# Row norm factors of a one-core decoder step: from a short column chain with diagonal products to one wide elementwise chain, with the side work emitted behind it

## The chip, the core and the metric

The kernel runs on one core of a Trainium2 chip. The metric is the device time of one execution in microseconds (us). Three executions of the kernel before took 1776.49, 1781.57 and 1782.59 us; their median, 1781.57 us, is the time before.

## What is computed

One inference step of a one-layer decoder for 512 prompt rows and 32 sample rows of width 1024. Of the reference only the norms matter here, and what stands around them:

```python
def rmsnorm(x, g):
    y = x * lax.rsqrt(jnp.mean(x * x, axis=-1, keepdims=True) + EPS)
    return y * g

ua, va, q, k, v, qi, ki, wi = split_proj(rmsnorm(xp, norm_mix_g) @ w_in)
ya, vn = gmlp_mix(...)                       # spatial gating
yb = dsa_prompt(...)                         # index scores, top-k mask, attention
xp = xp + concatenate([ya, yb]) @ w_out
xp = xp + mem_attend(rmsnorm(xp, norm_mem_g), mk, mv, mem_wq, mem_wo)
xp = xp + peer_apply(rmsnorm(xp, norm_ffn_g), ...)   # product keys, 16384 experts
y  = rmsnorm(xp, final_norm_g)
# the same for the 32 sample rows, with paged caches
```

## The kernel before, in words

Activations lie transposed: features on the 128 partitions (8 tiles, `kt`), rows along the free axis. `project` (L244) multiplies weight tiles with them; each product is three matmuls of split operands (`mm3`, L256 to L260), and each weight tile is first split by ScalarE (L220) and VectorE (L224). Three PSUM buffers (tag `pa`) hold products until `emit` reads them on VectorE.

A norm's gain is folded into the activations (`scaled`, L199 and L200), and the row factor 1/rms is applied when a product is read: `rb`, a tile that holds the factor of each row on every partition, is multiplied in at L410 (first projection), L557 (memory query), L595 and L612 (expert input and expert query). So products may start before `rb` is known, but at most three of them, since none can be read before `rb` is there.

`rb` is worked out five times for many rows: once in `folded` (544 rows, the start of the program) and four times in `norm` within `half` (256 or 288 rows, before the memory attention and before the expert layer, for each half of the rows). Each time:

- `squares4` (L146) squares the eight tiles and adds them over the partitions with ones, four tiles in four strips of 32 partitions: 32 equal rows in each of four strips.
- `turned` (L158) copies that to SBUF (L162) and multiplies with one column of `fold` (L166), which puts the sums of 128 rows on 128 partitions, one column for each 128 rows.
- `row_factors` (L170) first emits side work (`self.tick(self.NORM)`, 12 us worth of it), then copies the columns (L179, L180 or L182), works out the factor on 2 to 5 columns (`rstd`, L116 to L126: VectorE, a square root on ScalarE at L118, VectorE), multiplies the identity with each column (L192), multiplies ones with each of these diagonals (L193), and copies the result to `rb` (L194).

The memory's norm and the sample rows' last norm use `row_factors` as well and are not touched by the change.

Order. Side work (index scores and top-k masks, sample attention, routing) is written as generators. `tick(us)` steps them while main work is emitted, so that the program text mixes them; a scheduler with a simulated timeline then sets each engine's order from that text. An engine runs its list in order. Two places matter below: the first norm, whose ScalarE list also issues the DMAs of the cached index pages (`index_rows`, L1328); and the last one (second half, expert layer), where the side work is the routing of the first 128 rows (`top16`, L933 to L945, on VectorE).

Of the kernel before, what the change touches and what calls it, by code (L numbers as in the profile page):

```python
# [13 lines left out]
ALU = mybir.AluOpType  # L14
# [4 lines left out]
P = 128  # L19
NP = 512  # L20
NS = 32
NT = NP + NS
KT = 8
NB = 3
ND = NB * P
EPS = 1e-6
# [25 lines left out]
class Kernel:  # L52
# [102 lines left out]
                               for c, q in enumerate(self.sq4)])  # L155


    def turned(self, room, st, w):  # L158
        s = self.t(room, [P, w], tag="nsqs", bufs=4)
        n = w // len(st)  # L160
        for i, ps in enumerate(st):
            self.nc.scalar.copy(s[:, i * n : i * n + n], ps[:, :n])  # L162
        o = self.pst("pb")
        for b in range(0, w, P):
            m = min(P, w - b)
            self.nc.tensor.matmul(o[:m, b // P : b // P + 1], s[:, b : b + m], self.fold[:, :1], start=True, stop=True)  # L166
        return o


    def row_factors(self, pool, st, w, rb):  # L170
# [32 lines left out]
    def folded(self, pool, src, gain, w, parts, rb, room=None):  # L203
        nc = self.nc
        st = self.pst("pc") if room else [self.pst("pc") for _ in range(2)]
        for kt in range(KT):
            x = self.t(pool, [P, w], tag="fx", bufs=4 if w > NP else 2)
            nc.sync.dma_start(x, src[:, kt, :])
            g = gain[:, kt : kt + 1]
            for hi, lo, cs in parts:  # L210
                self.scaled(hi[:, kt, :], lo[:, kt, :], x[:, cs], g)
            if room:
                self.squares(room, x, kt, st, w, 1)
            else:
                self.squares4(pool, x, kt, st, w)
        self.row_factors(pool, st if room else self.turned(pool, st, w), w, rb)


    def split(self, hi, lo, x):
# [294 lines left out]
    def half(self, k, pw, h, uT, qT):  # L514
        nc, I = self.nc, self.I
        hh, hl = h
        w = 2 * P + k * NS
# [11 lines left out]
        xT, pm = yield  # L529
        nc.sync.dma_start(xT, I["xT"][:, :, cols])  # L530
        tmp = self.t(pm, [P, 7 * w])
        room = Room(tmp)
        rb = self.t(room, [P, w], tag="nrb")
# [6 lines left out]
        def norm(n, hh=hh, hl=hl):  # L540
            for kt in range(KT):
                self.scaled(hh[:, kt, :], hl[:, kt, :], xT[:, kt, :], self.gains[:, n, kt : kt + 1])
            self.row_factors(pm, self.turned(room, st, w), w, rb)

        st = [self.pst("pc")]
        self.project(pw, I["wO"], range(8), part, residual)
        yield
        norm(1)
        yield
        mst = ExitStack()  # L550
# [13 lines left out]
        for h in range(4):  # L564
            ps = self.pst("pa")
# [4 lines left out]
        pm = yield  # L570
        if not k:
            tmp = self.t(pm, [P, 7 * w])
        room = Room(tmp)
        rb = self.t(room, [P, w], tag="nrb")
        st = [self.pst("pc")]
        self.project(pw, I["wMO"], range(8), part, residual, kts=4)
        yield
        if k:
            nc.scalar.dma_start(self.x2[:, :, P:], xT[:, :, loc])
            nc.vector.tensor_copy(self.s_x, xT[:, :, 2 * P :])  # L580
        else:
            nc.scalar.dma_start(self.x2[:, :, :P], xT[:, :, P:])
            for kt in range(KT):
                self.natural(self.g_acc[:, kt, :], xT[:, kt, :P])
            norm(2)
        if k:
            pf = self.pool("pa_fold", stack=mst)
            fold = [self.t(pf, [P, KT, w], F32R) for _ in range(2)]
            part = [(*fold, cols)]
            norm(2, *fold)  # L590
# [1288 lines left out]
```

## Time and profile before

| | |
|---|---|
| runs | 1776.49, 1781.57, 1782.59 us |
| profiled execution | 1771.42 us, of which the span of the profile is 1769.7 us |
| TensorE (PE) busy | 1647.2 us, 93% of the span |
| VectorE (DVE) busy | 1476.1 us, 83% |
| ScalarE (ACT) busy | 863.9 us, 49% |
| granted TensorE clock | 0.966 of full speed on average |

The profiled execution lies 10.15 us below the median of the runs. The page's busy shares are averages over stages; the stages around the five norms have to be read one by one.

### The profile page before, as it was taken

Reading aid. Unit: us, or ns where it says so; the run is one execution under the profiler, and the core shown is the slowest. Engines: PE = TensorE matmul, PEld = TensorE weight load, DVE = VectorE, ACT = ScalarE, POOL = GpSimd, SP = SyncE. Lnnn points to the kernel's source line nnn. Section 1 sums busy time; section 2 is a strip of 40 time slices with the busy share of each in tenths; the row PEclk is TensorE's granted clock in tenths of the full one; section 3 lists DMA queues with packets and bytes.
Section 4 is the critical chain, followed back from the end, with each engine's and each line's share of the span. In section 5 each row is a group of like instructions: output and inputs, shape, how many; then the busy total and the mean of one; then the engine's idle time right before and its main releaser. Section 6 shows DMA issues by size and latency. Waiting matters only on the chain.

```text
span 1769.7 us, 29580 instructions
## 1 busy us (share of the span) xinstructions
PE 1647.2 (93%) x10238; PEld 1454.7 (82%) x10238; DVE 1476.1 (83%) x3654; ACT 863.9 (49%) x1585; POOL 499.2 (28%) x437
## 2 busy tenths in 40 slices
PE   5999879989997997999899998999999999999996
PEld 4879847879877896899889987888788888888885
DVE  4486989657669999999999975899897988878888
ACT  4246675866444336664774773333443333333333
POOL 2011024310000144232123222343333434345343
PEclk8999869999998998999999999999999999999998
DMA  6423236565754597999688779899998999999986
GB/s 210 116 77 116 79 91 209 179 211 157 229 168 137 168 360 277 328 340 335 211 297 323 268 276 298 277 346 328 374 350 303 372 358 324 354 328 326 362 304 241
DMA packets 195205, 460.33 MB, mean 260 GB/s; under 512 B 17976, under 2 KB 98616, under 8 KB 193648
## 3 DMA queue, kind: packets, MB, share of 16 engines
q1 hardware_dynamic: 127968, 239.59, 40.5%
q0 software_dynamic: 53072, 207.71, 33.1%
q10 hardware_dynamic: 14016, 11.15, 2.0%
q8 instruction: 80, 1.31, 0.3%
q14 instruction: 69, 0.57, 0.1%
HBM read 416.11 MB, written 42.05 MB: 259 GB/s over the span
## 4 chain that ended last, share of the span: by engine, by line
PE 66%; DVE 17%; DMA 6%; issue 6%; ACT 4%; POOL 1%; ACTq 0%; SPq 0%; POOLq 0%; DVEq 0%
PE t L260 20%; PE t L258 20%; PE t L259 20%; DVE t L224 3%; DMA t<-in_u,t 2%; DVE t L1744 2%; DMA t<-in_uT 1%; POOL t L1285 1%; PE t L654 1%; DMA wd<-t 1%; DVE t L942 1%; DVE t L937 1%; ACT t L220 1%; DVE t L945 1%; DVE t L933 1%
## 5 line engine op out<-in xcount | busy, mean ns | idle before, releaser
L260 PE MATMUL t<-t,t 128*128 128x384 f32 (+3 forms) x2544 | 867.6, 345 | 26.5 <-DVE t L224 26.0
L259 PE MATMUL t<-t,t 128*128 128x384 f32 (+3 forms) x2544 | 866.0, 342 | 0.0
L258 PE MATMUL t<-t,t 128*128 128x384 f32 (+3 forms) x2544 | 777.5, 345 | 12.4 <-ACT t L220 10.5
L220 ACT CAST t<-t 128x1024 fp32r<-128x1024 f32 (+4 forms) x512 | 418.5, 842 | 680.3 <-PE t L259 487.7
L224 DVE TENSOR_TENSOR t<-t,t 128x1024 fp32r<-128x1024 f32 (+4 forms) x512 | 487.5, 962 | 123.9 <-ACT t L220 120.4
L260 PEld LDWEIGHTS t<-t,t 128*128 128x128 f32 x2544 | 484.3, 191 | 76.0 <-DVE t L224 34.9
L258 PEld LDWEIGHTS t<-t,t 128*128 128x128 f32 x2544 | 484.2, 191 | 54.6 <-ACT t L220 15.3
L259 PEld LDWEIGHTS t<-t,t 128*128 128x128 f32 x2544 | 485.2, 191 | 39.9 <-issue 7.1
L1285 POOL DMA_INDIRECT t<-in_u,t x160 | 201.1, 1257 | 499.3 <-DVE t L1744 256.5
L1285 POOL DMA_INDIRECT t<-in_v,t x160 | 211.7, 1323 | 301.4 <-DVE t L1749 232.4
L1749 DVE SCALAR_TENSOR_TENSOR t<-t,t,t 128x1024 f32<-128x1024 f32 x160 | 204.7, 1279 | 3.9 <-DMA t<-in_v,t 3.0
L1744 DVE SCALAR_TENSOR_TENSOR t<-t,t 128x1024 f32<-128x1024 f32 x160 | 193.9, 1218 | 12.9 <-DMA t<-in_u,t 12.8
L1090 ACT ACTIVATE t<-t 128x512 f32<-128x512 f32 x96 | 96.9, 1147 | 28.5 <-DMA wd<-t 24.2
L1285 POOL DMA_INDIRECT t<-in_cK,t x32 | 31.4, 982 | 163.9 <-PE t L1504 86.6
L1226 DVE TENSOR_TENSOR t<-t,t 128x352 f32<-128x352 f32 x128 | 66.4, 520 | 7.2 <-DMA t<-gd 3.6
L1106 ACT ACTIVATE t<-t 128x384 f32<-128x384 f32 x128 | 62.2, 486 | 15.0 <-PE t L260 9.2
L1080 ACT ACTIVATE t<-t,t 128x128 f16<-128x128 f16 x192 | 58.8, 395 | 7.3 <-DVE t L1076 5.1
L704 ACT ACTIVATE t<-t,t 128x384 f32<-128x384 f32 x64 | 42.7, 667 | 31.8 <-DVE t L701 19.9
L1087 PE MATMUL t<-t,t 128*128 128x128 f16 x384 | 52.8, 225 | 4.8 <-DVE t L1077 2.6
L1088 PE MATMUL t<-t,t 128*128 128x128 f16 x384 | 51.2, 225 | 1.6 <-DVE t L1082 1.2
L1285 POOL DMA_INDIRECT t<-in_cV,t x32 | 34.2, 1069 | 56.2 <-PE t L1561 33.0
L1087 PEld LDWEIGHTS <-t 128*128 128x128 f16 x384 | 36.5, 100 | 12.0 <-issue 5.3
(400 smaller groups left out, 1416.6 us busy)
## 6 DMA issues: line engine op xcount, KB each, us to landing
t<-in_uT SPq DMA_DIRECT2D x128, 512.0 KB, 5.9
t<-in_v SPq DMA_DIRECT2D x128, 512.0 KB, 6.6
wd<-t POOLq DMA_DIRECT2D x11, 2048.0 KB, 9.1
t<-wd SPq DMA_DIRECT2D x32, 704.0 KB, 8.0
gd<-t SPq DMA_DIRECT2D x56, 192.0 KB, 4.4
t<-gd SPq DMA_DIRECT2D x56, 192.0 KB, 7.5
t<-in_wA SPq DMA_DIRECT2D x19, 512.0 KB, 5.6
t<-in_wO SPq DMA_DIRECT2D x16, 512.0 KB, 4.1
```

Of the source, the lines that this page charges most:

```text
L220: self.nc.scalar.copy(hi, x)
L224: self.pin_v = self.nc.vector.tensor_tensor(lo, x, hi, ALU.subtract)
L258: mm(out, ah, bh, start=first, stop=False)
L259: mm(out, ah, bl, start=False, stop=False)
L260: self.pin = mm(out, al, bh, start=False, stop=last)
L1087: nc.tensor.matmul(o, oj[:, x, :], oh[:, x, :], start=True, stop=False)
L1090: nc.scalar.activation(wb[:, :, t : t + 4].rearrange("p i t -> p t i"), ps.rearrange("p (t i) -> p t i", t=4), AF.Copy, scale=1.0 / 2048.0)
L1106: nc.scalar.activation(G, ps, AF.Gelu_apprx_tanh)
L1226: nc.vector.tensor_tensor(q(w)[:, : 4 * NB - 1], self.wp[:, :, i % 4, :], q(G)[:, : 4 * NB - 1], ALU.mult)
L1285: self.nc.gpsimd.indirect_dma_start(out=out, out_offset=None, in_=src, in_offset=bass.IndirectOffsetOnAxis(ap=ix, axis=0))
L1744: nc.vector.scalar_tensor_tensor(r, r, 1.0, hf, ALU.mult, ALU.mult, accum_out=a[:, k : k + 1])
L1749: nc.vector.scalar_tensor_tensor(acc, r, a[:, k : k + 1], acc, ALU.mult, ALU.add)
```

## The change

`turned` goes, and with it `row_factors` for these five norms. `wide_factors` copies the squares' sums as before, multiplies them with a full square of ones (one product of up to 288 columns: it adds the 4 x 32 rows, so every partition holds 32 times the sum of each row), and works out the factor elementwise on all 128 partitions and all columns: a scale and add that reads PSUM, a square root on ScalarE, a reciprocal, a square on ScalarE, and two fused steps of Newton's correction. There are no diagonals and no copy to `rb`; the chain writes `rb` itself. For the 544 rows of the first norm it runs twice, on 272 columns each. `tick(NORM)` stands behind the chain instead of in front of it.

```diff
-    def turned(self, room, st, w):
+    def wide_factors(self, room, st, w, rb):
+        nc = self.nc
         s = self.t(room, [P, w], tag="nsqs", bufs=4)
+        v = self.t(room, [P, w], tag="nsqs", bufs=4)
+        t = self.t(room, [P, w], tag="nsqs", bufs=4)
         n = w // len(st)
         for i, ps in enumerate(st):
-            self.nc.scalar.copy(s[:, i * n : i * n + n], ps[:, :n])
-        o = self.pst("pb")
-        for b in range(0, w, P):
-            m = min(P, w - b)
-            self.nc.tensor.matmul(o[:m, b // P : b // P + 1], s[:, b : b + m], self.fold[:, :1], start=True, stop=True)
-        return o
+            c = slice(i * n, i * n + n)
+            nc.scalar.copy(s[:, c], ps[:, :n])
+            o = self.pst("pb")
+            nc.tensor.matmul(o[:, :n], self.ones, s[:, c], start=True, stop=True)
+            self.factors(v[:, c], t[:, c], o[:, :n], NS, rb[:, c])
+        self.tick(self.NORM)
+
+    def factors(self, v, t, ps, n, rb):
+        nc = self.nc
+        nc.vector.tensor_scalar(v, ps, 1.0 / (n * KT * P), EPS, ALU.mult, ALU.add)
+        nc.scalar.sqrt(rb, v)
+        nc.vector.reciprocal(rb, rb)
+        nc.scalar.square(t, rb)
+        nc.vector.scalar_tensor_tensor(t, t, -0.5, v, ALU.mult, ALU.mult)
+        nc.vector.scalar_tensor_tensor(rb, t, 1.5, rb, ALU.add, ALU.mult)
...
-        self.row_factors(pool, st if room else self.turned(pool, st, w), w, rb)
+        if room:
+            self.row_factors(pool, st, w, rb)
+        else:
+            self.wide_factors(pool, st, w, rb)
...
-            self.row_factors(pm, self.turned(room, st, w), w, rb)
+            self.wide_factors(room, st, w, rb)
```

The new instructions have the lines 175 to 180 of the changed file, and every other line below stands 16 further down there. How the lists of the engines change is shown at three places.

**ScalarE, the first norm.** Before: the copy of the sums, the cast of a weight tile, DMAs of index pages (each is a TENSOR_LOAD of the page number, an address and the DMA), the square root's table and the square root on 5 columns.

```order
L162 COPY t_264<-t_182 128x272
L162 COPY t_264<-t_183 128x272
L220 CAST t_451<-t_425 128x1024
...
L118 ACT_TABLE_LOAD
L118 ACTIVATE t_279<-t_277 128x5
L1326 TENSOR_LOAD t_123
```

Now two square roots (L176) and two squares (L178) of 272 columns:

```order
L236 CAST t_428<-t_402 128x1024
...
L176 ACT_TABLE_LOAD
L176 ACTIVATE t_159<-t_265 128x272
L1342 TENSOR_LOAD t_123
L1344 ISA
L1344 DMA t_139<-in_cI 64x128
L176 ACTIVATE t_159<-t_265 128x272
...
L178 ACTIVATE t_266<-t_159 128x272
...
L178 ACTIVATE t_266<-t_159 128x272
L1342 TENSOR_LOAD t_123
```

Page DMAs stand between the chain's steps: one between the two square roots, two between the second root and the first square, one between the squares. Before the table load there are two in place of three.

**VectorE, the last norm.** Before, from the last weight split ahead of the chain to the first read of a product with `rb` (L612); the lines 933 to 945 are routing.

```order
L224 TENSOR_TENSOR t_6983<-t_6980,t_6982 128x1024
L179 COPY t_6784<-t_6659 128x2
...
L126 TENSOR_TENSOR t_6798<-t_6792,t_6794 128x3
...
L192 TENSOR_SCALAR t_6801<-t_60,t_6798 128x128
L192 TENSOR_SCALAR t_6804<-t_60,t_6798 128x128
...
L192 TENSOR_SCALAR t_6807<-t_60,t_6798 128x128
...
L194 COPY t_5145<-t_6800 128x288
...
L612 TENSOR_TENSOR t_5145<-t_6881,t_5145 128x288
```

Now (the routing lines are 949 to 961 there, L628 is the old L612, L611 the old L595):

```order
L175 TENSOR_SCALAR t_5105<-t_6579 128x288
L177 RECIPROCAL t_5105<-t_5105 128x288
L949 MAX t_6614<-t_6589 128x8 x8
L240 TENSOR_TENSOR t_6934<-t_6931,t_6933 128x1024
...
L179 SCALAR_TENSOR_TENSOR t_5105<-t_5105 128x288
...
L180 SCALAR_TENSOR_TENSOR t_5105<-t_5105 128x288
...
L611 SCALAR_TENSOR_TENSOR t_5105<-t_5103,t_66,t_5105 128x288
...
L628 TENSOR_TENSOR t_5105<-t_6778,t_5105 128x288
```

Routing stands in and behind the chain. Between the weight split and the first L612 there were 49 routing instructions of `top16`; now 45 stand between the same two (one L940 and three L937 fewer).

**TensorE, the start of the side work.** Before, the index weights' transposes (L425), the ones product of the sample scores (L1355) and the first mask score (L654):

```order
L425 MATMUL t_759<-t_60,t_638 128x8
L1355 MATMUL t_862<-t_860,t_58 128x256
L258 MATMUL t_1277<-t_152,t_1249 128x256
...
L654 MATMUL t_868<-t_167,t_151 128x256
```

Now (L441, L1371 and L670 are the same three):

```order
L441 MATMUL t_733<-t_60,t_615 128x8
L276 MATMUL t_1254<-t_152,t_1227 128x256
...
L441 MATMUL t_736<-t_60,t_615 128x8
L1371 MATMUL t_839<-t_837,t_58 128x256
L670 MATMUL t_845<-t_167,t_151 128x256
```

Ahead of the first mask score stood 292 projection matmuls (L258 to L260), now 325. Ahead of the last sample score (L1376) stood 576, now 624. Both lists have all of that side work within the first 912 of them. The orders differ in many small places up to about TensorE's row 4394 of 9635, and are the same behind it.

## Rows read from the trace of the kernel before

**Rows 1.** The page: span, busy time of the two busiest engines (us, share, instructions), and the chain that ended last by engine.

```profile
span 1769.7 us, 29580 instructions
...
PE 1647.2 (93%) x10238; PEld 1454.7 (82%) x10238; DVE 1476.1 (83%) x3654; ACT 863.9 (49%) x1585; POOL 499.2 (28%) x437
...
PE 66%; DVE 17%; DMA 6%; issue 6%; ACT 4%; POOL 1%; ACTq 0%; SPq 0%; POOLq 0%; DVEq 0%
```

**Rows 2.** Busy time by stretch: from:to and length in us, then busy us (and instructions) of PE, PE's weight loads, DVE, ACT and POOL, the granted PE clock, the DMA share and GB/s.

```profile
30.00:40.00 10.00, 5.55 (x21) 4.96 (x22) 4.67 (x19) 1.49 (x2) 2.11 (x3) 0.54 0.46 127
140.00:150.00 10.00, 8.64 (x45) 7.11 (x45) 5.13 (x14) 6.65 (x15) 0.00 (x0) 0.67 0.19 53
200.00:250.00 50.00, 37.08 (x197) 24.70 (x198) 45.59 (x260) 37.84 (x118) 11.40 (x12) 0.58 0.29 87
420.00:430.00 10.00, 9.81 (x85) 8.77 (x87) 8.15 (x25) 8.26 (x20) 0.00 (x0) 1.00 0.38 105
440.00:450.00 10.00, 10.00 (x81) 9.68 (x74) 6.51 (x16) 3.09 (x5) 0.00 (x0) 1.00 0.66 210
530.00:540.00 10.00, 1.93 (x9) 1.82 (x10) 10.00 (x52) 1.43 (x5) 0.00 (x0) 0.63 0.23 66
540.00:550.00 10.00, 9.84 (x63) 9.41 (x63) 10.00 (x48) 4.48 (x11) 0.00 (x0) 0.86 0.22 57
1000.00:1700.00 700.00, 689.33 (x3439) 596.37 (x3438) 593.97 (x921) 279.41 (x408) 261.76 (x204) 1.00 0.94 331
```

**Rows 3.** Timeline of the first norm: start and duration in us, engine (ACTq is ScalarE's issuing of DMAs), line, operation, and in brackets the idle time before and what ended it.

```profile
27.45 0.68 ACT L162 COPY t<-t 128x272 f32<-128x272 f32 x2 [4.38 <-PE t L153]
28.74 1.10 PE L166 MATMUL t<-t,t 128*128 128x1 f32 x10
29.11 1.23 DVE L224 TENSOR_TENSOR t<-t,t 128x1024 fp32r<-128x1024 f32 x1 [6.03 <-ACT t L220]
30.80 1.28 ACT L118 ACT_TABLE_LOAD   x1 [1.72 <-DMA t<-in_cI]
32.34 7.59 ACTq L1328 DMA_DIRECT2D t<-in_cI  x8
33.79 2.96 PE L193 MATMUL t<-t,t 128*128 128x128 f32 x10 [3.95 <-DVE t L192]
36.93 1.12 DVE L410 TENSOR_TENSOR t<-t,t 128x256 f32<-128x256 f32 x3
37.41 0.61 PE L258 MATMUL t<-t,t 128*128 128x288 f32 x1 [0.66 <-DVE t L410]
```

**Rows 4.** Prices: groups by line and shape, with count, busy us and mean ns of one, then the idle time before them.

```profile
L787 PE MATMUL t<-t,t 128*128 128x256 f32 x32 | 8.6, 385 | 1.2 <-ACT t L794 1.2
L148 ACT ACTIVATE t<-t 128x288 f32<-128x288 f32 x16 | 7.1, 441 | 0.6 <-DVE t L536 0.6
L410 DVE TENSOR_TENSOR t<-t,t 128x288 f32<-128x288 f32 x19 | 8.6, 451 | 21.4 <-PE t L260 21.4
L595 DVE SCALAR_TENSOR_TENSOR t<-t,t,t 128x288 f32<-128x288 f32 x8 | 4.0, 505 | 0.0
L871 DVE TENSOR_SCALAR t<-t 128x1 f32<-128x1 f32 x32 | 4.3, 140 | 0.0
L875 DVE RECIPROCAL t<-t 128x1 f32<-128x1 f32 x32 | 5.1, 159 | 3.2 <-ACT t L873 3.1
L1001 DVE RECIPROCAL t<-t 128x8 f32<-128x8 f32 x4 | 0.8, 195 | 0.0
```

**Rows 5.** Timeline of the second norm (first half, memory attention), columns as in rows 3; L1553 transposes and L1531 exponentials belong to the sample attention that runs beside it.

```profile
361.67 1.28 ACT L118 ACT_TABLE_LOAD   x1
364.12 1.28 ACT L1531 ACT_TABLE_LOAD   x1
366.28 0.66 PE L1553 MATMUL t<-t,t 128*128 128x128 f32 x4 [2.60 <-ACT t L1531]
```

**Rows 6.** Timeline of the last norm (second half, expert layer), columns as in rows 3. Between the first two PE rows lie 18 more projection matmuls of the same shape.

```profile
516.63 0.40 ACT L162 COPY t<-t 128x288 f32<-128x288 f32 x1 [1.66 <-PE t L153]
516.99 0.29 PE L259 MATMUL t<-t,t 128*128 128x288 f32 x1
519.50 0.29 PE L258 MATMUL t<-t,t 128*128 128x288 f32 x1
519.63 1.23 DVE L224 TENSOR_TENSOR t<-t,t 128x1024 fp32r<-128x1024 f32 x1 [3.74 <-ACT t L220]
522.14 0.87 DVE L933 MAX8 t<-t 128x8 f32<-128x128 f32 x4
527.41 0.61 PE L193 MATMUL t<-t,t 128*128 128x128 f32 x4
535.71 0.45 DVE L194 COPY t<-t 128x288 f32<-128x288 f32 x1
538.11 0.81 DVE L612 TENSOR_TENSOR t<-t,t 128x288 f32<-128x288 f32 x2
538.48 0.47 PE L753 MATMUL t<-t,t 128*128 128x128 f32 x1 [6.76 <-ACT t L600]
538.61 0.61 PE L258 MATMUL t<-t,t 128*128 128x288 f32 x1
```

**Rows 7.** Waits of 200 to 250 us: who waited for whom, total us, times, longest us.

```profile
PE t L889 <- ACT t L1508: 7.6, 2, 6.7
```

## The prediction

> **What bounds the kernel now.** I read the page first, for the span and the chain [rows 1]: TensorE is busy 93% of it and carries 66% of the chain, so what shortens the time either takes work from TensorE where it never stops, or takes away a wait of TensorE elsewhere. Then the stretches [rows 2], to see which of the two holds at each of the five norms. From 1000 to 1700 us TensorE is busy 689.33 of 700 us, and both lists are the same there, so nothing can come from that part. Around the third and fourth norm (420 to 430 and 440 to 450 us) it is busy 9.81 and 10.00 of 10: only its own work counts. At the first norm (30 to 40 us) it is busy 5.55 of 10 at a granted clock of 0.54, and at the last (530 to 540 us) 1.93 of 10, while VectorE is busy 10.00 of 10. Last I read the timelines of the first, second and last norm [rows 3, 5, 6], for what ends the wait, and the price rows [rows 4].
>
> **First norm (27 to 37 us).** The sums are copied at 27.45; TensorE stops after the column products (28.74 + 1.10) and gets its next projection product at 37.41, when the first L410 has read a PSUM buffer [rows 3]. Now two products of ones take the place of L166: nearest row 128x256, two records for a product, 32 records in 8.6 busy us with overlap, so about 0.45 us for 272 columns [rows 4]. TensorE is done at 28.74 + 0.9 = 29.65. Wide steps cost about 0.45 us on VectorE (L410, 288 columns from PSUM, 0.451), 0.5 for a fused step (L595, 0.505) and 0.44 on ScalarE (L148, 0.441) [rows 4]; queued behind each other the fused ones take nearer 0.45. VectorE: first scale at 29.2, the weight split of 1.23 us that stands between, second scale done at 31.3. ScalarE: the table of 1.28 us goes one page DMA earlier, so it is in by about 31.1, and the first root is done at 31.5, the second at 32.2. Behind that ScalarE's list has page DMAs, 0.95 us each (8 in 7.59 us) [rows 3]: two before the first square (33.4 to 33.85), one more before the second (34.4 to 34.85). VectorE then does two fused steps (to 34.8) and a third (to 35.35), and L410 of 0.45 frees the buffer at 35.85. Against 37.41: **1.5 us earlier**. What is left of the stop is about as long as before, so I take the low clock behind it as unchanged.
>
> **Second norm (350 to 368 us).** TensorE waits here for the sample attention's exponentials, which stand on ScalarE behind the square root's table (361.67) and their own table (364.12); the transposes start at 366.28 after a wait of 2.60 us [rows 5]. In the new list the square stands ahead of the second table, so this wait ends one ScalarE step of 0.44 us later: **0.4 us lost**. The saved column and diagonal products lie in the wait and count nothing.
>
> **Third and fourth norm (420 to 450 us).** TensorE never waits, so its own products count. Four L166 and four L193 records for 256 rows, six of each for 288, start some 0.1 us apart or a little more (ten L166 in 1.10 [rows 3], four L193 in 0.61 [rows 6]): 0.9 and 1.15 us. One wide product in their place takes 0.45. **1.1 us saved** for the two. The longer elementwise chain is covered by three products of 24 matmuls of 0.13 us (19 intervals from 516.99 to 519.50 [rows 6]), 9 us; without that cover it would cost its own 3 us. No side work is running at these two, so the moved tick emits nothing.
>
> **Last norm (516 to 538 us).** `rb` is there at 536.1 (535.71 + 0.45), L612 starts at 538.11 and TensorE's projection goes on at 538.61 [rows 6]. From the root on VectorE is never idle in between, so L612 starts when what stands ahead of it in VectorE's list is through. By the new list I count, from the weight split at 519.63: scale to 521.2, root on ScalarE to 521.75, reciprocal to 522.25, eight L933 of 0.2 (four in 0.87 [rows 6]), a split, four other routing steps of 0.26, the fused step, and so on: `rb` is finished near 529.7 in place of 536.1, but 25 routing steps, a split and two L595 still stand between it and L612, which starts at 537.1. That is 1.0 us earlier, and just the four routing steps that moved behind it. They still have to be done in a stretch where VectorE stays full (10.00 of 10 up to 550 us [rows 2]), so I count half: **0.5 us saved**. The 12 us of routing that are now emitted behind the chain are thus not behind it on the engine: the scheduler has mixed them in again.
>
> **The unknown price** is a reciprocal of 256 to 288 columns. The trace has 1 column at 159 ns and 8 at 195 ns [rows 4]. Lower bound: it runs like other wide VectorE steps, 0.45 us. Upper bound: the slope of these two rows, 36 ns for 7 columns, 5.1 ns each: 288 columns 1.6 us. I take 0.45, because a plain step of one column (L871) already takes 140 ns [rows 4], so that a row of 195 ns for 8 columns is mostly start, and keep 1.6 for the range: at the second norm that is 1.2 us more, at the first 0.8, at the last 0.6, nothing at the other two.
>
> [...]
>
> **Sum.** -1.5 + 0.4 - 1.1 - 0.5 = -2.7 us. Against the profiled execution, 1771.42 us, that is 1768.7; this execution lies 10.15 us below the median of the runs, so on their scale 1781.57 - 2.7 = **1778.9 us**. About 0.3%, 5.3 us, is what a measurement can tell from no change, so the likeliest case is no difference that shows.
>
> **Rivals.**
> - *A wait on index pages goes too* (faster). From 140 to 150 us TensorE is busy 8.64 of 10 at a clock of 0.67 [rows 2]: 1.36 us idle and some 3.3 us of work at the lower level. The last sample score now stands behind 624 projection matmuls in place of 576, so pages have longer to land. If the stop goes, 4.6 us more are saved: 1774.3. Against it: the pages may land as much later.
> - *The side work starts too late* (slower). The first mask score stands 33 matmuls later, 4.4 us at 0.132, the last sample score 48, 6.3 us; the first norm gives back 1.5. From 200 to 250 us TensorE is busy only 37.08 of 50 at a clock of 0.58 [rows 2], waiting for just these chains. If they set the end of that stretch, their 6.3 us replace the 1.5 saved: 6.3 + 0.4 - 1.1 - 0.5 = +5.1, 1786.7. It decides from the point where the sample chain starts over 1.5 us later than now.
> - *The wide reciprocal is slow*, 1.6 us: -2.7 + 2.6 = -0.1, 1781.5.
>   [...]
> - *The change does not shorten the chain*: at the first norm the page DMAs hold ScalarE as long as the diagonals held TensorE, and at the last one L612 starts where it did. Then 1781.57 - 1.1 + 0.4 = 1780.9.
>
> **How the numbers follow.** Chances: forecast 0.38, index pages 0.25, late side work 0.25, slow reciprocal 0.08, no shorter chain 0.04. The order is redrawn in many small places up to about 1000 us; one wait like L889 for L1508 in the middle stretch, 6.7 us at the longest [rows 7], may come or go anywhere, so each case spreads by some 6 us to either side. Faster by over 0.3% (below 1776.2): 0.3 of the forecast, 0.7 of the pages, a tenth of the rest: 0.33. Slower by over 0.3% (above 1786.9): a tenth of the forecast, 0.55 of the late side work, a quarter of the rest: 0.21. Within: 0.46. The range goes from the pages' case less its spread, 1768, to a little under the late side work plus its spread, 1791.
>
> **What would show it.** First norm: L410 starts near 35.4, with page DMAs between the squares. Second: the exponentials' transposes start 0.4 us later against the table load. Third and fourth: the same TensorE list with one product in place of four or six pairs. Last: `rb` done near 530, L612 near 537 on the same scale, VectorE full throughout. The reciprocal's own row settles its price. Wrong would be: TensorE taking up its products at 530 (then a wait of 8 us was ahead of L612, not work), a reciprocal above 1.6 us, a granted clock of 1.00 at 30 to 40 us, or a difference over 5 us that arises between 140 and 350 us.

## The result: slower by 1.0%, and the profile after

The changed kernel takes 1796.32 us (median of 6 runs, 1792.73 to 1800.66) against 1779.16 us before (6 runs, 1774.52 to 1782.59): ratio **1.0098**, 95% interval 1.0081 to 1.0115, **17 us slower**. The profiled execution took 1794.08 us. In the changed kernel the lines after the new functions stand 16 further down: L258 to L260 are L274 to L276, L410 is L426, L612 is L628, L1077 is L1093.

The page, to hold against [rows 1]: the engines' busy times moved by 8 us at most, the span is 22.7 us longer.

```profile
span 1792.4 us, 29454 instructions
...
PE 1652.6 (92%) x10189; PEld 1455.6 (81%) x10190; DVE 1484.0 (83%) x3616; ACT 866.4 (48%) x1590; POOL 495.2 (28%) x437
```

Stretches of the changed kernel, columns as in [rows 2]. At 140 to 150 us the wait on index pages is gone and the clock is full; the first norm holds TensorE longer; from 1000 us on nothing differs. The row of 690 to 790 us is the one to remember.

```profile
30.00:40.00 10.00, 2.66 (x12) 2.35 (x11) 8.03 (x12) 3.19 (x6) 1.05 (x2) 0.61 0.50 141
140.00:150.00 10.00, 10.00 (x81) 9.48 (x79) 2.60 (x12) 4.84 (x13) 0.00 (x0) 1.00 0.23 65
200.00:250.00 50.00, 36.26 (x184) 25.61 (x184) 44.25 (x246) 33.99 (x104) 12.24 (x12) 0.53 0.30 87
690.00:790.00 100.00, 76.71 (x564) 70.83 (x563) 97.81 (x286) 65.99 (x123) 32.15 (x27) 0.90 0.85 301
1000.00:1700.00 700.00, 690.35 (x3499) 599.58 (x3498) 596.07 (x930) 289.32 (x429) 259.37 (x202) 1.00 0.93 329
```

The same 100 us in the kernel before: TensorE is busy 5.6 us more.

```profile
690.00:790.00 100.00, 82.31 (x592) 77.36 (x591) 98.62 (x285) 66.41 (x111) 35.96 (x29) 0.93 0.82 298
```

The wide reciprocal by shape (count | busy us, mean ns of one | idle before). It costs 1.75 to 1.95 us, above the upper bound of 1.6: from 256 to 288 columns 208 ns more, 6.5 ns a column.

```profile
L177 DVE RECIPROCAL t<-t 128x288 f32<-128x288 f32 x2 | 3.9, 1954 | 1.8 <-ACT t L176 1.8
L177 DVE RECIPROCAL t<-t 128x272 f32<-128x272 f32 x2 | 3.6, 1822 | 0.7 <-ACT t L176 0.7
L177 DVE RECIPROCAL t<-t 128x256 f32<-128x256 f32 x2 | 3.5, 1746 | 0.0
```

The first norm, to hold against [rows 3]. ScalarE copies the sums 1.23 us later than before: four index pages' DMAs are issued ahead of it in both kernels, but here ScalarE's wait ends with the last of these DMAs and not with the sums. From there to TensorE's next projection product it is 8.97 us in place of 9.96, and 3.56 of these are the two reciprocals. (The start of this copy alone varies between 26.3 and 28.7 us in the profiles of all the runs below, 27.45 and 27.18 in two of before's own program, so the 1.23 us need not be the change's.) The first squares wait for them.

```profile
28.68 0.67 ACT L166 COPY t<-t 128x272 f32<-128x272 f32 x2 [5.16 <-DMA t<-in_cI]
...
34.46 0.43 ACT L178 ACTIVATE t<-t 128x272 f32<-128x272 f32 x1 [1.60 <-DVE t L177]
...
32.57 3.56 DVE L177 RECIPROCAL t<-t 128x272 f32<-128x272 f32 x2 [0.66 <-ACT t L176]
...
37.17 0.75 DVE L426 TENSOR_TENSOR t<-t,t 128x256 f32<-128x256 f32 x2
...
37.65 0.61 PE L274 MATMUL t<-t,t 128*128 128x288 f32 x1 [7.34 <-DVE t L426]
```

The second norm, to hold against [rows 5]: between the two table loads now stand the root, the wait for the reciprocal and the square. The transposes start 6.16 us after the first load in place of 4.61.

```profile
367.44 1.28 ACT L176 ACT_TABLE_LOAD   x1
...
369.22 1.75 DVE L177 RECIPROCAL t<-t 128x256 f32<-128x256 f32 x1
...
371.00 0.42 ACT L178 ACTIVATE t<-t 128x256 f32<-128x256 f32 x1
371.44 1.28 ACT L1547 ACT_TABLE_LOAD   x1
...
373.60 0.90 PE L1569 MATMUL t<-t,t 128*128 128x128 f32 x3 [3.48 <-ACT t L1547]
```

The last norm, to hold against [rows 6]. From the copy to the last fused step it is 14.3 us in place of 19.5, but L628, the first read of a product with `rb`, starts 21.64 us after the copy; L612, the same read, started 21.48 us after it: routing steps stand between, and the chain's end was not the bound.

```profile
528.67 0.40 ACT L166 COPY t<-t 128x288 f32<-128x288 f32 x1 [1.05 <-PE t L153]
...
533.78 1.95 DVE L177 RECIPROCAL t<-t 128x288 f32<-128x288 f32 x1 [0.51 <-ACT t L176]
...
542.55 0.44 DVE L180 SCALAR_TENSOR_TENSOR t<-t 128x288 f32<-128x288 f32 x1
...
550.31 0.82 DVE L628 TENSOR_TENSOR t<-t,t 128x288 f32<-128x288 f32 x2
```

At the third norm TensorE waits once, for a residual add (L552, L536 before) that VectorE has behind a wide reciprocal:

```profile
437.95 1.95 DVE L177 RECIPROCAL t<-t 128x288 f32<-128x288 f32 x1 [1.27 <-ACT t L176]
439.82 0.36 DVE L552 TENSOR_TENSOR t<-t,t 128x256 f32<-128x256 f32 x1
...
440.33 0.35 PE L274 MATMUL t<-t,t 128*128 128x256 f32 x1 [1.35 <-DVE t L552]
```

The norms account for little of the 22 us: the second loses 1.55 us, the third a wait of 1.35, the first and the last some 0.2 each. I therefore laid the starts of all 2544 first products of the projections (L258, now L274) of the two profiles side by side. The changed kernel is 7.3 us ahead at 148 us and level at 170; then it is behind by some 11 us at 400, 12 at 505, 15 at 685, 24 to 25 at 770, 21.5 from 1290 to the end. So two stretches carry the loss: **170 to 400 us** (side work of the attention) and **685 to 770 us** (expert layer). Of the five norms only the second, at 350 to 368 us, lies in one of them.

### The profile page after: what moved, and what is told of

It is laid out like the page before. It is cut to its first block, busy times and chain, and to the rows that moved or that the text cites. A ratio compares the mean times of both kernels' runs of the same rounds, so it can differ in the third digit from the quotient of the medians.

```text
span 1792.4 us, 29454 instructions
## 1 busy us (share of the span) xinstructions
PE 1652.6 (92%) x10189; PEld 1455.6 (81%) x10190; DVE 1484.0 (83%) x3616; ACT 866.4 (48%) x1590; POOL 495.2 (28%) x437
## 4 chain that ended last, share of the span: by engine, by line
PE 66%; DVE 18%; issue 5%; DMA 5%; ACT 5%; POOL 1%; ACTq 0%; SPq 0%; POOLq 0%; DVEq 0%
PE t L274 20%; PE t L276 20%; PE t L275 20%; DVE t L240 3%; DVE t L1760 2%; DMA wd<-t 2%; ACT t L236 1%; DMA t<-in_uT 1%; PE t L670 1%; DVE t L958 1%; DVE t L953 1%; POOL t L1301 1%; DVE t L961 1%; DVE t L1092 1%; DVE t L949 1%
## 5 line engine op out<-in xcount | busy, mean ns | idle before, releaser
L276 PE MATMUL t<-t,t 128*128 128x384 f32 (+3 forms) x2544 | 868.6, 346 | 11.3 <-DVE t L240 10.9
L274 PE MATMUL t<-t,t 128*128 128x384 f32 (+3 forms) x2544 | 778.0, 345 | 35.4 <-ACT t L236 25.2
L236 ACT CAST t<-t 128x1024 fp32r<-128x1024 f32 (+4 forms) x512 | 418.3, 842 | 700.8 <-PE t L275 476.7
L274 PEld LDWEIGHTS t<-t,t 128*128 128x128 f32 x2544 | 484.2, 191 | 84.7 <-ACT t L236 30.0
L276 PEld LDWEIGHTS t<-t,t 128*128 128x128 f32 x2544 | 484.5, 191 | 55.4 <-DVE t L240 16.5
L1301 POOL DMA_INDIRECT t<-in_u,t x160 | 196.6, 1229 | 500.2 <-DVE t L1760 267.1
L1760 DVE SCALAR_TENSOR_TENSOR t<-t,t 128x1024 f32<-128x1024 f32 x160 | 194.3, 1220 | 10.6 <-DMA t<-in_u,t 9.0
L1106 ACT ACTIVATE t<-t 128x512 f32<-128x512 f32 x96 | 97.2, 1147 | 27.9 <-DMA wd<-t 21.2
L1301 POOL DMA_INDIRECT t<-in_cV,t x32 | 34.1, 1066 | 58.8 <-PE t L1577 34.2
```

The source lines that it names most:

```text
L236: self.nc.scalar.copy(hi, x)
L274: mm(out, ah, bh, start=first, stop=False)
L276: self.pin = mm(out, al, bh, start=False, stop=last)
L1106: nc.scalar.activation(wb[:, :, t : t + 4].rearrange("p i t -> p t i"), ps.rearrange("p (t i) -> p t i", t=4), AF.Copy, scale=1.0 / 2048.0)
L1301: self.nc.gpsimd.indirect_dma_start(out=out, out_offset=None, in_=src, in_offset=bass.IndirectOffsetOnAxis(ap=ix, axis=0))
L1760: nc.vector.scalar_tensor_tensor(r, r, 1.0, hf, ALU.mult, ALU.mult, accum_out=a[:, k : k + 1])
```

## The experiments

Three theories. **P**, the place: side work is emitted behind the chain, so it starts late. **R**, the price: the wide chain costs what is lost, above all its reciprocal. **S**, the order: any edit lets the scheduler draw a new order of all engines up to about 1000 us, and this one is worse. Ratios are to runs of the kernel before on the same chip in the same session. Each ratio stands as it is on record with its interval; it is not the quotient of the two medians beside it, which differs from it by up to 0.0011 (e7: 1.0002 as a quotient).

| run | us | before | ratio | 95% interval |
|---|---|---|---|---|
| e1 old chain, tick behind | 1775.03 | 1776.11 | 1.0003 | 0.9982–1.0024 |
| e2 wide chain, tick in front | 1792.04 | 1776.11 | 1.0090 | 1.0049–1.0132 |
| e3 wide, no reciprocal | 1784.02 | 1776.11 | 1.0043 | 1.0021–1.0066 |
| e4 one more small copy | 1786.36 | 1776.11 | 1.0064 | 1.0037–1.0090 |
| e5 first norm alone | 1793.79 | 1778.60 | 1.0077 | 1.0054–1.0099 |
| e6 later norms alone | 1794.31 | 1778.60 | 1.0078 | 1.0044–1.0112 |
| e7 reciprocal root | 1778.95 | 1778.60 | 0.9991 | 0.9966–1.0015 |
| e8 NORM = 13 | 1778.08 | 1778.60 | 0.9991 | 0.9970–1.0011 |
| e9 wide, before's order | 1776.22 | 1774.93 | 1.0004 | 0.9986–1.0022 |
| e10 reciprocal root, before's order | 1772.29 | 1774.93 | 0.9975 | 0.9959–0.9992 |
| e11 reciprocal root, changed order | 1789.46 | 1774.93 | 1.0073 | 1.0054–1.0093 |
| e12 before, held | 1775.45 | 1774.93 | 1.0007 | 0.9990–1.0023 |
| e13 changed order to 565 us | 1785.42 | 1779.44 | 1.0034 | 1.0018–1.0049 |
| e14 changed order from 557 us | 1789.15 | 1779.44 | 1.0055 | 1.0032–1.0077 |
| e15 changed order to 400 us | 1784.96 | 1779.44 | 1.0038 | 1.0016–1.0059 |

**e1**, against before:

```diff
-        if w > NS:
-            self.tick(self.NORM)
...
             done += n
+        if w > NS:
+            self.tick(self.NORM)
```

> The short chain of before (turned, row_factors) with the call that pours out side work moved behind it: the place of the side work alone. Theory P (the place: side work is poured out later, and the mask scores, samples and attention that hang on it start and end later): 15 to 20 us over before, the first mask score some 4 us later. Theory R (the price of the wide chain, above all the reciprocal of 1.75 to 1.95 us): within 3 us of before. Theory S (every edit lets the scheduler draw a new order up to about 1000 us, and an order is worth some us either way by luck): anything within 20 us of before, without a first mask score that explains it.

Measured 1.0003: moving the call costs nothing. But it did not make the side work late either: TensorE's list stayed close to before's, with 292 projection matmuls ahead of the first mask score as before and that score at 68.5 us (68.8 before). So P falls as far as the place of the call goes; what lateness itself costs, e1 does not show.

**e2**, against the changed kernel:

```diff
+        self.tick(self.NORM)
         for i, ps in enumerate(st):
...
-        self.tick(self.NORM)
```

> The wide chain with the side work poured out in front of it as before: the chain alone. Theory P: within 3 us of before. Theory R: 15 to 20 us over before, as the whole change. Theory S: anything within 20 us of before.

Measured 1.0090, as the whole change. The loss comes with the wide chain, by its price (R) or by the order that it brings (S).

**e3**, against the changed kernel:

```diff
-        nc.vector.reciprocal(rb, rb)
+        nc.vector.tensor_scalar(rb, rb, 0.0, 0.02, ALU.mult, ALU.add)
```

> The whole change with the wide reciprocal replaced by a plain multiply and add to a constant (0.02), so the norm factors of the main rows are not those of the reference. Each replaced step should take some 0.43 us in place of 1.75 to 1.95. Theory R: 8 to 15 us under the whole change (five norms, each with 1.5 us less per reciprocal and two in a row in the first). Theory P: the late side work stays, 2 to 4 us under the whole change at most. Theory S: anything, the order is drawn anew if the scheduler knows the step's price.

(The factors are then a constant, so the run stands for its time alone.) Measured 1.0043: some 10 us under the changed kernel by the ratios, in R's range. But 8 us over before are left with no reciprocal at all, and the first mask score starts 3.0 us earlier than before, where the changed kernel has it 4.5 us later: a loss does not need a late mask score.

**e4**, against before:

```diff
             nc.vector.tensor_copy(ss, st[:, :nb])
+        if w > NS:
+            nc.vector.tensor_copy(ss[:, :1], ss[:, :1])
```

> Before, with one more 128x1 or so copy (a column of the row sums onto itself, some 0.15 us) in each norm of more than 32 rows: an edit that is worth under 1 us by itself. Theories P and R: within 2 us of before. Theory S: a new order, 5 to 20 us away in either direction.

Measured 1.0064, 11 us for one copy of 0.15 us in each of the five norms: S, for one redraw. With e3 it shows that an order is worth about as much as what is disputed, so single edits can't decide.

**e5** and **e6**, against the changed kernel (e5 the first edit, e6 the second; both also put `turned` back, which is cut here):

```diff
-            self.wide_factors(room, st, w, rb)
+            self.row_factors(pm, self.turned(room, st, w), w, rb)
```

```diff
-        if room:
-            self.row_factors(pool, st, w, rb)
-        else:
-            self.wide_factors(pool, st, w, rb)
+        self.row_factors(pool, st if room else self.turned(pool, st, w), w, rb)
```

> The wide chain (and the side work behind it) in the first norm alone; the four later norms keep before's short chain. The engine orders are the whole change's up to some 400 us, and before's nearly to the letter from there to 570 us. Theory S (the loss lies in the new order of 150 to 400 us, where TensorE's clock falls to half after waits at 370 and 395 us that before's order had too, but without the fall): 8 to 12 us over before at 400 us, and 6 to 14 us over it at the end. Theory R (the price of the wide chains, five times over): 3 to 5 us over before, the first norm's share.

> The other part: the wide chain in the four later norms alone. The orders are before's up to some 350 us and the whole change's from there to 950 us. Theory S: within 3 us of before at 350 us, the clock stays up until the second norm, and at the end 5 to 12 us over before, mostly from the stretch 690 to 790 us, where the whole change lost 9 us. Theory R: four reciprocals with the waits of their norms, 6 to 12 us, which lie at 360 to 370, 415 to 455 and 520 to 540 us.

Measured 1.0077 and 1.0078: 14 us each, and both together only 17. A price of five chains would add up. e5 comes in at the top of S's range, e6 over both theories' ranges, and in the profiles both lose some 8 us between 685 and 770 us, where neither has a norm.

**e7**, against the changed kernel:

```diff
-        nc.scalar.sqrt(rb, v)
-        nc.vector.reciprocal(rb, rb)
+        nc.scalar.activation(rb, v, AF.Abs_reciprocal_sqrt)
```

> The whole change with the square root on ScalarE and the reciprocal on VectorE replaced by one ScalarE activation, the reciprocal root, before the same Newton step. Theory R: it takes 0.43 us in place of some 0.43 + 1.8 us, so the first norm's chain is 3.5 us or more shorter, and the time is 0 to 5 us under before. Theory S: the first norm gives its 3 us, but the order is drawn anew and the end is within 15 us of before on either side.

Measured 0.9991. The projections are 4.4 us ahead at 68 us, and that is lost again behind it. Both theories had room for it; it leans to R.

**e8**, against before:

```diff
-    NORM = 12.0
+    NORM = 13.0
```

> Before, with the amount of side work that a norm pours out set to 13 in place of 12, and nothing else. The orders are before's up to 148 us, others from there to 400 us, and before's again after that. Theory S: 3 to 12 us over before, all of it between 150 and 400 us and seen as a clock at half speed or as waits of TensorE there. Theories P and R: within 2 us of before.

Measured 0.9991: no loss. S's expectation was wrong: this new order of 150 to 400 us is no worse. After eight runs neither theory was settled: e4 and the sum of e5 and e6 spoke against R, e8 against S, and e7 leaned to R.

**Holding the order.** What was missing is the same order with another chain, and another order with the same chain. For e9 to e15 every engine's list is held: each instruction gets a dependency on the one that is to stand ahead of it on its engine, for the order alone, without a semaphore.

```diff
+    for engine, order in json.loads(zlib.decompress(base64.b64decode(_ORDER))).items():
+        q = queues[engine]
+        for a, b in zip(order, order[1:]):
+            tc.add_manual_dep(q[b], q[a].name, mybir.DependencyInfo(mybir.DependencyClass.NoSync, mybir.DependencyReason.DATA), reason="order")
...
             Kernel(ctx, tc, I, O).build()
+            _in_order(tc, nc)
```

**e12** does that to before itself (its own order), **e9** to the wide chain in before's order. In e9 the tick is called between the products with ones and the elementwise steps, as in before between `turned` and the rest:

```diff
             nc.scalar.copy(s[:, c], ps[:, :n])
-            o = self.pst("pb")
-            nc.tensor.matmul(o[:, :n], self.ones, s[:, c], start=True, stop=True)
-            self.factors(v[:, c], t[:, c], o[:, :n], NS, rb[:, c])
-        self.tick(self.NORM)
+            sums.append((c, self.pst("pb")))
+            nc.tensor.matmul(sums[-1][1][:, :n], self.ones, s[:, c], start=True, stop=True)
+        self.tick(self.NORM)
+        for c, o in sums:
+            self.factors(v[:, c], t[:, c], o[:, :n], NS, rb[:, c])
```

> Before, word for word, with every engine's order held to the one that it has anyway: what holding an order costs by itself, and a second profile of before's program. All theories: within 3 us of before. The profile tells how far the stretch of 280 to 400 us, where before's first profile kept its full clock, differs from run to run of one program: if it is again at full clock there, the clock falls in the other kernels belong to their orders; if it falls here too, they are chance.

> The wide chain with its reciprocal (the part after the side work's call is emitted behind that call, which e1 found to be worth nothing), but every engine's order held to before's: each old instruction stands where it stood in before, the products with ones where the turning products stood, the wide steps where the short chain's steps stood. Theory S (the loss is the new order): within 5 us of before. Theory R (the loss is the chain's own price, above all the reciprocal): 10 to 17 us over before, as the whole change.

e12 1.0007: holding costs nothing that can be measured. **e9 1.0004: in before's order the wide chain with its slow reciprocals costs nothing that can be measured** (the ratio 1.0098 of the changed kernel lies far outside e9's interval, and e11 below has the changed order beside it in one session). R falls as the cause of the 17 us.

**e10** is e9, **e11** the changed kernel in its own order, both with e7's edit.

> As e9, with the reciprocal root on ScalarE in place of square root and wide reciprocal (as in e7). Theory S: 0 to 5 us under before, since the first norm's 4 us are kept and nothing is redrawn. Theory R: the same, 0 to 5 us under before, and 10 to 17 us under e9, where theory S has the two kernels within 6 us of each other.

> The whole change in its own order on every engine, held, with the reciprocal root on ScalarE in place of square root and wide reciprocal. Theory S: the order's loss stays, 8 to 17 us over before. Theory R: the loss goes with the reciprocal, within 4 us of before.

e10 0.9975, e11 1.0073. So the four corners are 1.0004 and 1.0098 with the reciprocal, 0.9975 and 1.0073 without: the order is worth 0.0094 and 0.0098, some **17 us**, whichever chain runs in it; the reciprocal 0.0029 and 0.0025, some **5 us**, whichever order it runs in. The order's worth is far outside the noise in both rows; the reciprocal's is about as large as the noise of either difference and rests on both agreeing. Three corners are held and of one session; the fourth, the changed kernel, is not held and of an earlier one. R's forecasts for e10 against e9 and for e11 both fail, S's hold. e10 also beats both kernels, by some 4 us against before.

**e13**, **e14** and **e15** hold e9's program to one order up to a cut and to the other behind it (the table of the diff above alone changes).

> e9's program (the wide chain) held to the changed kernel's order on every engine for what that kernel starts in its first 565 us, and to before's order for the rest. If the order loses in two places of its own (theory S in two parts), this run shows the early one: the two profiles differ by 10.6 us up to there, so 6 to 11 us over before, all of it by 565 us, and 690 to 770 us as in before. If the late loss follows from the early one: 13 to 17 us over before, with TensorE's waits of 8 to 10 us at 690 to 790 us.

> The reverse of e13: before's order for what starts in the first 557 us, the changed kernel's order for the rest. Two parts: 5 to 9 us over before, from the stretch of 690 to 770 us, with two waits of 8 to 10 us there. If the late loss follows from the early one: within 3 us of before.

> As e13 with the cut at 400 us in place of 565: the changed order of the first norm and of the mask scores, samples and attention behind it alone. Two parts: the same as e13 within 2 us (the profiles of the whole change and of e9 differ by 10.6 us by 400 us and by no more at 565). If the orders around the third to fifth norm (400 to 540 us) carry the early loss: within 3 us of before.

e13 1.0034, e15 1.0038, e14 1.0055. The early part costs some 6 us and lies before 400 us already; the late part some 10 us, and it needs no changed order ahead of it. Together 0.0089 of 0.0098. e13 came in at the bottom of its range and e14 just above the top of its own.

The waits of TensorE from 690 us on show that the late part is reproduced. Columns: who waited for whom, total us, times, longest. First e14 (before's early order, the changed order behind it; its lines stand 18 below before's):

```profile
PE t L1105 <- DVE t L1095: 12.0, 4, 9.9
PE t L276 <- ACT t L238: 9.5, 3, 8.4
```

The changed kernel has the same two:

```profile
PE t L1103 <- DVE t L1093: 11.9, 4, 9.9
PE t L274 <- ACT t L236: 9.6, 3, 8.5
```

e9, with the same chain and before's order, has neither, but one of 7.9 us (so has the kernel before, at 706 us):

```profile
PE t L278 <- DVE t L242: 14.3, 8, 7.9
PE t L1105 <- DVE t L1095: 2.1, 2, 1.8
```

Two waits of 9.9 and 8.4 us in place of one of 7.9 are some 10 us more, the size of the late part. TensorE's busy time from 690 to 790 us sorts by the order alone: 82.1 to 84.3 in the six profiles with before's order there (before, e9, e10, e12, e13, e15), 76.7 to 76.9 in the three with the changed one (changed kernel, e11, e14). e13 and e14 run one program, with the two orders the other way round (columns as in [rows 2]); first e13, then e14:

```profile
690.00:790.00 100.00, 82.34 (x589) 76.82 (x588) 96.86 (x290) 66.94 (x124) 32.57 (x27) 0.90 0.80 292
690.00:790.00 100.00, 76.67 (x572) 71.31 (x571) 94.27 (x280) 64.67 (x116) 29.56 (x26) 0.90 0.82 289
```

What these waits are, ScalarE's timeline of the changed kernel shows. L1106 belongs to `spread`, the step of the expert layer that lays out the routing weights in a tile (`wb`) and sends it to DRAM (`wd`). It stands at the head of ScalarE's list and waits 8.07 us for the transfer of the tile's old content to `wd`, since it is to fill the same tile again; the weight cast L236 stands behind it, and TensorE needs that cast.

```profile
774.39 0.48 ACT L1122 ACTIVATE t<-t 128x384 f32<-128x384 f32 x1
782.94 3.67 ACT L1106 ACTIVATE t<-t 128x512 f32<-128x512 f32 x4 [8.07 <-DMA wd<-t]
786.37 1.09 ACT L236 CAST t<-t 128x1024 fp32r<-128x1024 f32 x1
```

TensorE stands still for as long:

```profile
778.72 0.34 PE L276 MATMUL t<-t,t 128*128 128x384 f32 x1
787.51 0.69 PE L274 MATMUL t<-t,t 128*128 128x384 f32 x1 [8.45 <-ACT t L236]
```

In before's order the same instruction (L1090 there) waits for the same transfer too, but only 4.76 us, and TensorE's longest wait between 740 and 790 us is 1.6:

```profile
764.23 4.06 ACT L1090 ACTIVATE t<-t 128x512 f32<-128x512 f32 x4 [4.76 <-DMA wd<-t]
```

The other wait of the changed kernel is VectorE's list: L1093, which TensorE waits for, stands behind 9 us of routing steps, gathers' products and other steps of `spread`, VectorE never idle.

```profile
720.44 0.29 PE L1103 MATMUL t<-t,t 128*128 128x128 f16 x1 [9.95 <-DVE t L1093]
```

Of the early part the cause is settled only as far as the order. The falls of the clock at 374 and 398 us, of which the expectations of e5 and e12 speak, are no mark of it: between 290 and 420 us the lower level (a granted clock of 0.50, the lowest that any of these traces shows) takes 10.2 us in the changed kernel (3.4 and 6.8) and in e11, but also 10.2 in e14, which has before's order there, and 0 to 6.8 in the other profiles of before's order. They come and go from run to run. The stretch ahead of it, where the clock is low in both kernels (0.58 from 200 to 250 us before [rows 2], 0.53 after), is at most a lead: between 160 and 290 us the lower level takes 34.1 to 44.4 us in six profiles with before's order (before, e1, e9, e10, e12, e14; mean 39.2) and 37.5 to 47.8 in six with the changed one (changed kernel, e2, e5, e11, e13, e15; mean 44.9). The 5.7 us between the means would be up to 2.8 us of TensorE's work at that clock of 0.50, and the two groups overlap. The runs speak against the clock as the main part: their mean granted clock is 0.963 in e13 and e15, as in the runs of before beside them (0.963). A single profile is a weak witness for this stretch: e14, in before's order up to 557 us, is 5.3 us behind before at 400 us, and e8, whose runs lose nothing, 8.5. A late start of the side work is not excluded either: e13 and e15 have the first mask score at 72.3 us, behind 325 projection matmuls, as the changed order has it. How the 6 us divide into waits, displaced products and clock stays open.

## Why the prediction was wrong, point by point

The forecast was 1778.9 us, the range 1768 to 1791; the changed kernel's 1796.32 lie 5 us above it.

- **First norm, 1.5 us earlier.** Right in direction from the copy on, by 0.99 us, and mis-sized: the two reciprocals took 3.56 us where the sum had 0.9. TensorE goes on at 37.65 in place of 37.41 only because the copy started 1.23 us later in this profile. In before's order the same chain (e9) is longer than the old one, 10.6 us from the copy to the next product in place of 9.96; with the reciprocal root (e10) it is 7.6.
- **Second norm, 0.4 us lost.** Right in mechanism, the square ahead of the second table. Mis-sized: 1.55 us (6.16 less 4.61), since the reciprocal stands there too; the upper bound had said 1.2 more, that is 1.6.
- **Third and fourth norm, 1.1 us saved.** The products went as said, but the cover did not hold: at 439.0 us TensorE waits 1.35 us for a residual add that VectorE has behind a reciprocal of 1.95 us.
- **Last norm, 0.5 us saved.** Nothing: L628 starts 21.64 us after the copy, before it was 21.48. That L612 hangs on what stands ahead of it in VectorE's list, not on `rb`, was right.
- **The unknown price.** 0.45 us was taken, 1.75 to 1.95 measured; the reason given, that a row of 195 ns for 8 columns is mostly start, said nothing of 256 to 288 columns. The slope of the two rows, 5.1 ns a column, was near the 6.5 measured; a reciprocal above 1.6 us was one of the signs of being wrong, and it came.
- **The sum.** As a price of the norms alone it is not contradicted: with the slow reciprocal it read -0.1 us, and e9 measured 1.0004, which is +0.7 us (interval -2.5 to +3.9). The interval is wider than any term of the sum, so this confirms no single term; that it comes out although the first and the last norm did not is in part luck.
- **The step that failed** is the last one: "one wait like L889 for L1508 ... may come or go anywhere, so each case spreads by some 6 us to either side". The redrawn order went in as noise around zero, and it is the largest term, +17 us, in two pieces of +6 and +10. It is not symmetric either: of the redrawn orders measured (changed kernel, e1 to e8), six were slower by 0.4 to 1.0% and three the same within their intervals, none faster; why most were worse no run shows. From 690 to 790 us, where TensorE, VectorE and ScalarE wait for each other's lists, I had read no row, since no norm lies there.
- **Rivals.** The index pages' wait did go (10.00 of 10 busy at full clock), and TensorE was 7.3 us ahead at 148 us; at 170 us that was used up, because the side products displaced there came later. The late side work began as forecast, the first mask score 4.5 us later (4.4 forecast), and its +5.1 us is close to the early part's 6. But that is a size, and the mechanism is not shown: with the mask score early (e3) time is lost as well, and no run makes the side work late and nothing else (e1 was to do it, but its mask score is not late).
- **What would show it wrong** named a difference over 5 us between 140 and 350 us. It came: the changed kernel is 7.3 us ahead at 148 us and 5.8 behind at 350. But by e13 and e14 the larger piece, 10 of 16 us, arises past 557 us, where nothing was watched for.

## What to carry to other kernels

Where a scheduler draws the order, an edit has two prices, its own and the new order's, and the second can be felt far from the edit (here some 10 us past 557 us, behind the last of the five norms: e14); look up the stretches where several engines wait for each other's lists, whether or not the edit lies there. To measure the first price, hold the order on every engine by order-only dependencies and change the chain alone; to measure the second, hold the chain and swap orders, whole and up to a cut. Held to the old order, an edit that seemed to cost 1% cost nothing that could be measured, and its better form (one reciprocal root in place of root and reciprocal) gained 0.25%.

## What was not expected of the hardware

- A reciprocal of 128 partitions takes 1.75, 1.82 and 1.95 us for 256, 272 and 288 columns, where a plain step of the same shape (L175) takes 0.43, 0.44 and 0.46 us. A reciprocal root on ScalarE takes 0.43 and 0.41 us for 272 columns (L176 of e7).
- One program in one order varies a good deal: the 108 runs of the kernel before that stand beside e1 to e15 lie between 1766.7 and 1788.1 us, and they are the shorter the higher the mean granted clock (0.960: 1780.9 us, mean of 8; 0.967: 1769.9, mean of 5). Its profiled execution of 1771.42 us and e12's of 1762.52 lie 8 and 13 us under the medians, so differences of up to 3 us in one stretch of two profiles were not read as causes.
